# Hybrid attention and state-space trunk: states in the ring of attention outputs, states made one half projection sooner, the last two input tiles by token halves, gate inputs loaded through the ring

## The chip, the core and the metric

The kernel runs on one core of one Trainium2 chip. The core has a matrix engine (TensorE, PE in the profile, with its weight loads as PEld), a vector engine (VectorE, DVE), a scalar engine (ScalarE, ACT), a general engine (GpSimd, POOL) and a queue that here issues every DMA (SyncE, SP). Each engine takes its own instructions in the order in which they stand in its queue; they wait for each other by semaphores. The metric is the device time of one execution in microseconds (us), the median of several runs. One execution is also taken by the hardware profiler; all start times below count from the beginning of its span.

## The reference

Two decoder layers on x of 1024 tokens by 1024 channels in float32, the first with dilated window attention, the second with a state space layer. The change lies in the second:

```python
def s5_mixer(h, w_in, a_re, a_im, log_dt, b_re, b_im, c_re, c_im, d_skip, w_glu, b_glu, w_out):
    proj = h @ w_in
    u, z = proj[..., :SSM_WIDTH], proj[..., SSM_WIDTH:]
    y = s5_scan(u, a_re, a_im, log_dt, b_re, b_im, c_re, c_im, d_skip)
    g = jax.nn.gelu(y)
    y = g * jax.nn.sigmoid(g @ w_glu + b_glu)
    return (y * jax.nn.silu(z)) @ w_out
...
x = x + rms_norm(h, ssm_post_norm[j])
```

`s5_scan` is a linear recurrence over the tokens with 64 complex states for each of 64 groups of 16 channels.

## The kernel before

Matrix products are made in float32 accuracy from two rounded parts of each operand: a helper, `split` (line 80), casts a tile to its high part on ACT (L86) and subtracts that from the tile on another engine, mostly DVE (L87), for the low part. Each product is then three matmuls (`proj_part`, L113): high by high, high by low, low by high.

The second layer has three stages. **Input projection with the state space work** (`layer1`): the projection has 16 column tiles of weights (0 to 7 give `u`, 8 to 15 give `z`), each for two halves of 512 tokens. A half projection is 24 matmuls into one bank of PSUM (`psj`); 32 of them are made in a row by `in_order`. Between them the code interleaves the state space work of 8 groups, each 128 channels wide, by a table: a list `at` gives for each half projection t the stages to be run behind it. The stages of a group e are: its loads (`ssm_loads`: BT, Cg, Sg), the load of its input U from DRAM, where the projection's halves were written (`ssm_input`), of the taps and CA (`ssm_taps`), the states (`ssm_states`) and the outputs (`ssm_outputs`). `ssm_states` makes 8 matmuls `pv` (L1380), then on DVE and POOL a rotation (L1381 to L1384), a scan along the blocks (L1387), and a rotation back (L1389 to L1393) into X. `ssm_outputs` makes 16 matmuls `py` from U with the taps (L1407) and X with CA (L1408), then the gelu on ACT, POOL and DVE (L1409 to L1414, all named Y) and writes Y to DRAM (`y_dr`, L1415). A tile X holds half a group; its pool has two buffers for the tag, so one group's states.

**The gate projection** (`glu`): g is read back from `y_dr`, with tokens and channels in other places, in 16 loads `gy` (8 groups by two token halves, L1476), each split into its high and low part: `g0b` is the first half's pair of tiles, `g1b` the second half's. The loads take their places from a ring of small buffers (`slot`). Then 8 column tiles of `w_glu` by two halves are made. `in_order` begins this stage with a block (start="block"): two weight tiles by two halves in four banks (`psb`), seven of eight groups deep first, the eighth at the end. The weights of a tile are loaded, cast (`whi`) and subtracted (`wlo`) two tiles ahead, since there are two buffers of each.

**The output projection** with the norm and the residual (`out_tiles`).

Large tiles have tags b0 to b5, each a buffer that is used again: `h1` (the normalised input of the layer) is in b4 and b5 for the first token half, in b0 and b2 for the second; the taps are in b1 (groups 0 to 3) and b3 (4 to 7); g is in b1 and b3 for the first half, in b4 and b5 for the second. The ring of attention outputs (pool `outs`, tag O) has four buffers of 128 by 1024 values; in the second layer only the last norm's weights (`post`) use it.

A scheduler sets each engine's order from the order of the code, from priorities (`high_priority`) and from its own clock; `issue_after` holds an instruction behind another one.

Of the kernel before, what the change touches and what calls it, by code (L numbers as in the profile page):

```python
# [15 lines left out]
F32 = mybir.dt.float32  # L16
# [7 lines left out]
P = 128  # L24
S = 1024
D = 1024
KT = 8
H = 512
# [88 lines left out]
def proj_half(c, w, h):  # L117

    pool, tag = ((c.psj, "psj"), (c.pst, "pst"))[c.banks % 2]
    c.banks += c.wide  # L120
    ps = pool.tile([P, H], F32, tag=tag, name="psj")
    proj_part(c, ps, w, h, range(KT))
    return ps
# [643 lines left out]
def in_order(c, srcs, h, use, after=None, start=None, ws=()):  # L767

    t = 0

    def one(e, th, ps):
        nonlocal t
        use(e, th, ps)
        if after:
            after(t)
        t += 1

    ws = list(ws) or [load_w(c, srcs[e]) for e in range(2 if start else 0)]  # L780
    if start == "block":
        jobs = [(e, th) + ((c.psj, "psj"), (c.psl, "psl"))[th] for th in range(2) for e in range(2)]
        pss = [pool.tile([P, H], F32, tag=tag, name="psb") for _, _, pool, tag in jobs]
        for ks in (range(KT - 1), (KT - 1,)):
            for ps, (e, th, _, _) in zip(pss, jobs):
                proj_part(c, ps, ws[e], h[th], ks)
                if ks[0]:
                    one(e, th, ps)
    elif start == "half":
        for e in range(2):  # L790
            one(e, 0, proj_half(c, ws[e], h[0]))
        pss = [c.psj.tile([P, H], F32, tag="psj", name="psj") for _ in range(2)]
        for part in range(2):
            cs = slice(part * 256, part * 256 + 256)
            for e in range(2):
                proj_part(c, pss[e][:, cs], ws[e], [x[:, :, cs] for x in h[1]], range(KT), part == 0)
                if part:
                    one(e, 1, pss[e])
    c.wide = 1 if start == "half" else c.wide
    for e in range(len(ws), len(srcs)):  # L800
        w = load_w(c, srcs[e])
        for th in range(2):
            one(e, th, proj_half(c, w, h[th]))
    c.banks = c.wide = 0

# [562 lines left out]
def ssm_states(self):  # L1368

    c, et, BT, Cg, Sg = self.c, self.et, self.BT, self.Cg, self.Sg  # L1370
    nc = c.nc
    U = self.U
    lo, hi = slice(0, 64), slice(64, 128)
    self.X = []
    for b in range(2):
        gs = slice(b * 4, b * 4 + 4)
        T1, T2, X = (c.ssm.tile([P, 4, P], F32, name=n, tag=n, bufs=2) for n in ("T1", "T2", "X"))
        pv = c.psl.tile([P, 4, P], F32, tag="psl", name="pv")
        for j in range(4):
            nc.tensor.matmul(pv[:, j, :], BT[:, b * 4 + j, :], U[:, b * 4 + j, :], start=True, stop=True)  # L1380
        nc.vector.tensor_tensor(T1, Cg[:, gs], pv, op=ALU.mult)  # L1381
        nc.vector.tensor_tensor(T2[lo], Sg[lo, gs], pv[hi], op=ALU.mult)
        nc.vector.tensor_tensor(T2[hi], Sg[hi, gs], pv[lo], op=ALU.mult)
        nc.gpsimd.tensor_tensor(T1, T1, T2, op=ALU.add)  # L1384
        for j in range(4):
            g = et * 8 + b * 4 + j
            nc.vector.tensor_tensor_scan(T1[:, j], c.rho[:, g:g + 1].to_broadcast([P, P]),  # L1387
                                         T1[:, j], 0.0, op0=ALU.mult, op1=ALU.add)
        nc.gpsimd.tensor_tensor(X[:, :, 1:P], Cg[:, gs, 0:P - 1], T1[:, :, 0:P - 1], op=ALU.mult)  # L1389
        nc.gpsimd.memset(X[:, :, 0:1], 0.0)  # L1390
        nc.vector.tensor_tensor(T2[lo], Sg[lo, gs], T1[hi], op=ALU.mult)
        nc.vector.tensor_tensor(T2[hi], Sg[hi, gs], T1[lo], op=ALU.mult)  # L1392
        nc.vector.tensor_tensor(X[:, :, 1:P], X[:, :, 1:P], T2[:, :, 0:P - 1], op=ALU.subtract)  # L1393
        self.X.append(X)


def ssm_outputs(self):
# [20 lines left out]
def y_view(c, et, th):  # L1418

    return bass.AP(c.y_dr.tensor, c.y_dr.offset + et * P * S + th * 4 * 16384, [[P, P], [16384, 4], [1, P]])  # L1420


def layer1(c, a, h1, ws):

    nc, tc = c.nc, c.tc
    c.ssm = c.es_pa.enter_context(tc.tile_pool(name="ssm", bufs=1, side="left", reuse_waits="tile"))
    def use_u(et, th, ps):
        ut = c.slot("ut")
        with tc.high_priority(AHEAD):
            nc.scalar.copy(ut.rearrange("p (i n) -> p i n", i=4)[:, ::-1, :], ps.rearrange("p (i n) -> p i n", i=4))  # L1430
            dst = bass.AP(c.u_dr.tensor, c.u_dr.offset + et * P * S + (1 - th) * 4 * 16384, [[P, P], [16384, 4], [1, P]])
            nc.sync.dma_start(dst, ut.rearrange("p (i n) -> p i n", i=4))

    def use_z(et, th, ps):
        z = c.slot("z1")
        with tc.high_priority(AHEAD):
            nc.scalar.activation(z, ps, AF.Tanh, scale=0.5)
            nc.vector.scalar_tensor_tensor(z, z, 1.0, ps, op0=ALU.add, op1=ALU.mult)
            nc.sync.dma_start(c.z_dr[et, :, th * H:th * H + H], z)

    groups = [Ssm(c, a, e) for e in range(8)]
    c.taps = []
    at = [[] for _ in range(40)]
    for e in range(8):
        t = (11 * e + 2) // 4
        for stage, d in ((ssm_loads, (-1, 2)[e] if e < 2 else 3), (ssm_input, 5), (ssm_taps, 6), (ssm_states, 7), (ssm_outputs, 10)):
            at[t + d + 1].append((stage, e))

    def run(t):
        for stage, e in at[t + 1]:  # L1450
            if stage is ssm_loads and e == 1:
                with tc.issue_after(groups[0].load_U.ins):
                    stage(groups[e])
            else:
                stage(groups[e])

    def use(e, th, ps):
        (use_u if e < 8 else use_z)(e % 8, th, ps)

    run(-1)  # L1460
    in_order(c, [a["ssm_w_in"][e] for e in range(16)], h1, use, run, start="half", ws=ws)
    for t in range(32, 39):
        run(t)


def glu(c, a):
    nc, tc = c.nc, c.tc
    bh = c.cst.tile([P, KT], F32, name="bh")
    nc.sync.dma_start(bh, a["b_glu"])
    nc.vector.tensor_scalar(bh, bh, 0.5, None, op0=ALU.mult)  # L1470
    g, y2 = [], []
    for th, tags in enumerate((("b1", "b3"), ("b4", "b5"))):
        g.append([c.pb.tile([P, KT, H], F32R, tag=t, name=f"g{th}{t}") for t in tags])
        for et in range(8):
            y = c.slot("gy")
            nc.sync.dma_start(y.rearrange("p (i n) -> p i n", i=4), y_view(c, et, th))  # L1476
            split(c, g[th][0][:, et, :], g[th][1][:, et, :], y)
    y2.append([c.pb.tile([P, KT, H], F32R, tag=t, name=f"y0{t}") for t in ("b0", "b2")])

# [16 lines left out]
def trunk(tc, a):  # L1496
# [6 lines left out]
    with ExitStack() as es:  # L1503
# [51 lines left out]
                          z112.rearrange("p (k x) -> p k x", k=8))  # L1555
        h1, ws = attn_out(c, a, g, raw)
        c.es_pa.close()
        layer1(c, a, h1, ws)
        c.es_pa.close()
        c.pa2 = c.es_pa.enter_context(tc.tile_pool(name="pa2", bufs=1, side="left", reuse_waits="tile"))  # L1560
        y2 = glu(c, a)

        w = [[c.pa2.tile([P, KT, H], F32R, tag=f"w0{x}", name=f"wf0{x}") for x in "hl"],
             [c.pb.tile([P, KT, H], F32R, tag=t, name=f"wf1{t}") for t in ("b1", "b4")]]
# [99 lines left out]
```

## Time and profile before

| what | us |
|---|---|
| median of 3 runs (1678.32 to 1683.48) | 1678.59 |
| the profiled execution's own time | 1679.3 |
| its span | 1677.5 |
| first layer, and the start of the second: 0 to 1250 (PE busy) | 1250 (1239.88) |
| projection before the first states: 1250 to 1298 (PE busy) | 48 (46.83) |
| projection with states and outputs: 1298 to 1480 (PE busy) | 182 (178.51) |
| first block of the gate projection: 1480 to 1512 (PE busy) | 32 (27.87) |
| rest of the gate projection: 1512 to 1581 (PE busy) | 69 (68.67) |
| output projection and the end: 1581 to 1677 (PE busy) | 96 (88.37) |

PE's instructions overlap: a matmul of 512 columns is shown as 0.4 us long, and the next one begins 0.23 us after it, so a hole in PE is read best from starts. A row of the profile such as "PE py L1408 <- DVE X L1393: 2.4, 1, 2.4" says that PE waited before its instructions of line 1408 for X of line 1393 on DVE: us in total, times, longest. Buffer numbers are left out of names, so T1 and T2 are T, Y1 and Y2 are Y, g0b1 and g0b3 are g0b. The granted clock of PE (PEclk) is 1 at full speed.

### The profile page before, as it was taken

Reading aid. Unit: us, or ns where it says so; the run is one execution under the profiler, and the core shown is the slowest. Engines: PE = TensorE matmul, PEld = TensorE weight load, DVE = VectorE, ACT = ScalarE, POOL = GpSimd, SP = SyncE. Lnnn points to the kernel's source line nnn. Section 1 sums busy time; section 2 is a strip of 40 time slices with the busy share of each in tenths; the row PEclk is TensorE's granted clock in tenths of the full one; section 3 lists DMA queues with packets and bytes.
Section 4 is the critical chain, followed back from the end, with each engine's and each line's share of the span. In section 5 each row is a group of like instructions: output and inputs, shape, how many; then the busy total and the mean of one; then the engine's idle time right before and its main releaser. Section 6 shows DMA issues by size and latency. Waiting matters only on the chain.

```text
span 1677.5 us, 26337 instructions
## 1 busy us (share of the span) xinstructions
PE 1650.1 (98%) x9714; PEld 1390.6 (83%) x9714; DVE 1011.9 (60%) x2509; ACT 712.2 (42%) x1730; POOL 460.0 (27%) x303
## 2 busy tenths in 40 slices
PE   8999999999999999999999999999999999999998
PEld 6889999978888888888888888887788887867886
DVE  8698898625554554545455455557562888845533
ACT  5232223236455464645546464654452223343411
POOL 2000000131241514324161441404220344513121
PEclk9999999999999999999999999999999999989999
DMA  6213455531232414233252423318346979365432
GB/s 238 86 49 109 144 181 158 170 109 55 79 99 82 119 54 114 68 90 95 67 139 65 120 79 87 109 34 234 103 162 175 273 222 259 101 207 171 144 120 86
DMA packets 176857, 212.19 MB, mean 126 GB/s; under 512 B 37443, under 2 KB 133462, under 8 KB 176728
## 3 DMA queue, kind: packets, MB, share of 16 engines
q1 hardware_dynamic: 176728, 210.52, 42.3%
q8 instruction: 76, 1.25, 0.3%
q14 instruction: 53, 0.43, 0.1%
HBM read 153.51 MB, written 56.96 MB: 125 GB/s over the span
## 4 chain that ended last, share of the span: by engine, by line
PE 87%; DVE 7%; DMA 3%; issue 1%; POOL 1%; ACT 1%; SPq 0%; DVEq 0%; ACTq 0%; POOLq 0%
PE psj L113 46%; PE psq L376 11%; PE psl L474 5%; PE pso L551 4%; PE pt L502 4%; PE pso L886 3%; PE pso L885 3%; PE pso L884 3%; PE pso L577 1%; PE psb L113 1%; DVE T L1387 1%; PE psv L237 1%; DVE T L1392 1%; PE psv L236 1%; PE psv L235 1%
## 5 line engine op out<-in xcount | busy, mean ns | idle before, releaser
L113 PE MATMUL psj<-hh,wlo 128*128 128x512 f32 x896 | 358.2, 400 | 0.0
L113 PE MATMUL psj<-hh,whi 128*128 128x512 f32 x896 | 358.1, 400 | 0.0
L113 PE MATMUL psj<-hl,whi 128*128 128x512 f32 x896 | 355.2, 396 | 0.0
L87 POOL TENSOR_TENSOR wlo<-wraw,whi 128x1024 fp32r<-128x1024 f32 x48 | 115.2, 2399 | 395.9 <-ACT whi L86 380.8
L113 PEld LDWEIGHTS psj<-hh,whi 128*128 128x128 f32 x896 | 168.8, 188 | 37.0
L113 PEld LDWEIGHTS psj<-hh,wlo 128*128 128x128 f32 x896 | 168.8, 188 | 36.4
L113 PEld LDWEIGHTS psj<-hl,whi 128*128 128x128 f32 x896 | 168.7, 188 | 36.3
L491 ACT ACTIVATE lg<-lg,nm 128x128 f32<-128x128 f32 (+1 forms) x384 | 168.2, 442 | 37.3 <-DVE nm L486 37.3
L480 DVE CUSTOM_DVE_ANT_0 lg<-psl,T 128x128 f32<-128x128 f32 (+1 forms) x384 | 110.5, 347 | 88.7 <-PE psl L474 88.7
L86 ACT CAST whi<-wraw 128x1024 fp32r<-128x1024 f32 x80 | 83.7, 1046 | 163.8 <-PE psj L113 117.5
L376 PE MATMUL psq<-whi,v 128*128 128x256 f32 x640 | 120.3, 284 | 0.0
L87 DVE TENSOR_TENSOR ph<-pt,ph 128x512 fp32r<-128x512 f32 (+2 forms) x160 | 96.7, 622 | 15.3 <-ACT ph L86 13.1
L113 PE MATMUL psj<-h1h,whi 128*128 128x512 f32 (+1 forms) x272 | 105.0, 387 | 0.9 <-ACT h1h L86 0.9
L87 DVE TENSOR_TENSOR kl<-psj,kh 128x512 fp32r<-128x512 f32 x48 | 33.2, 692 | 120.1 <-ACT kh L86 119.5
L113 PE MATMUL psj<-h1l,whi 128*128 128x512 f32 (+1 forms) x272 | 104.1, 383 | 0.2 <-DVE h1l L87 0.2
L113 PE MATMUL psj<-h1h,wlo 128*128 128x512 f32 (+1 forms) x272 | 104.1, 383 | 0.0
L86 ACT CAST ph<-pt 128x512 fp32r<-128x512 f32 (+2 forms) x160 | 81.6, 530 | 46.5 <-PE pt L502 45.5
L376 PEld LDWEIGHTS psq<-whi,v 128*128 128x128 f32 x640 | 100.0, 189 | 1.2 <-issue 1.2
L376 PE MATMUL psq<-wlo,v 128*128 128x256 f32 x320 | 91.2, 286 | 0.7 <-DVE wlo L87 0.7
L551 PE MATMUL pso<-ph,vs 128*128 128x256 f32 (+1 forms) x544 | 86.6, 284 | 0.0
L502 PE MATMUL pt<-identr,lg 128*128 128x128 f32 x560 | 82.2, 276 | 0.0
L1253 POOL TENSOR_TENSOR Ks<-Ks,O 128x16 f32<-128x16 f32 x8 | 3.7, 462 | 284.0 <-ACT Ks L1251 284.0
(284 smaller groups left out, 3688.6 us busy)
## 6 DMA issues: line engine op xcount, KB each, us to landing
wraw<-in_w_in_dram SPq DMA_DIRECT2D x56, 512.0 KB
mw<-wt_dr SPq DMA_DIRECT2D x48, 256.0 KB
v<-in_w_v_dram SPq DMA_DIRECT2D x20, 512.0 KB
vp<-v_dr SPq DMA_DIRECT2D x16, 512.0 KB
wraw<-in_ssm_w_in_dram SPq DMA_DIRECT2D x16, 512.0 KB
v_dr<-v SPq DMA_DIRECT2D x30, 256.0 KB
rot_dr<-rt SPq DMA_DIRECT2D x48, 128.0 KB
ca_dr<-ca SPq DMA_DIRECT2D x32, 144.0 KB
```

What stands on the lines that cost most here:

```text
L86: c.last_hi = nc.scalar.copy(hi, src).ins
L87: return (engine or nc.vector).tensor_tensor(lo, src, f32(hi), op=ALU.subtract)
L113: nc.tensor.matmul(ps, a[:, s], b[:, k, :], start=first and k == 0 and n == 0, stop=k == KT - 1 and n == 2, skip_group_check=True)
L376: nc.tensor.matmul(o, r[x][:, k, ts], w[y][:, k, :], skip_group_check=True, start=i in (0, 4, 5) and t % 2 == k == n == 0, stop=k == 3 and ...
L474: nc.tensor.matmul(psl[:, h, o], x[HEADS[h], qs], y[HEADS[h], ks], start=j == js[0] and n == 0, stop=n == 2, skip_group_check=True)
L480: nc.vector.tensor_tensor_reduce(lg[:, h, j, 0:w], psl[:, h, o], bt[:, h, 256 - w:256], scale=1.0, scalar=-3.0e38, op0=ALU.add, op1=ALU.ma ...
L491: nc.scalar.activation(lg[:, h, j, 0:w], lg[:, h, j, 0:w], AF.Exp, bias=nm[:, h, b:b + 1], accum_out=ms[:, col:col + 1])
L502: c.nc.tensor.transpose(pt[:, n * P:(n + 1) * P], lg[:, h, j, part * P:part * P + P], c.ident)
L551: nc.tensor.matmul(o, l, r, start=n == 0, stop=n == len(jobs) - 1, skip_group_check=True)
L884: nc.tensor.matmul(ps, gh[:, k, ts], wh[:, k, :], start=n == 0, stop=False)
L885: nc.tensor.matmul(ps, gh[:, k, ts], wl[:, k, :], start=False, stop=False)
L886: nc.tensor.matmul(ps, gl[:, k, ts], wh[:, k, :], start=False, stop=n == KT - 1)
```

## The change

Four edits. X of a group becomes one buffer of the ring of attention outputs (both halves of the group in it), so up to four groups' states can stand at once. In the table, the input's load and the states of groups 1 to 7 move one half projection up. `in_order` makes the last two tiles of the input projection by token halves: both tiles' first half, then both tiles' second. And the 16 loads `gy` go through three buffers of the ring of attention outputs, six places, held behind the last group's load of U; g gets other buffers: b1 and b4 for the first half, b5 and b3 for the second.

```diff
@@ in_order
-    c.wide = 1 if start == "half" else c.wide
-    for e in range(len(ws), len(srcs)):
+    c.wide = int(start == "half")
+    pairs = 2 if start == "half" else 0
+    for e in range(len(ws), len(srcs) - pairs):
         w = load_w(c, srcs[e])
         for th in range(2):
+            one(e, th, proj_half(c, w, h[th]))
+
+    ws = [(e, load_w(c, srcs[e])) for e in range(len(srcs) - pairs, len(srcs))]
+    for th in range(2):
+        for e, w in ws:
             one(e, th, proj_half(c, w, h[th]))
@@ ssm_states
-    self.X = []
+
+    X2 = c.outs.tile([P, D], F32, tag="O", name="X", bufs=4).rearrange("p (b g n) -> p b g n", b=2, g=4)
+    self.X = [X2[:, b] for b in range(2)]
     for b in range(2):
         gs = slice(b * 4, b * 4 + 4)
-        T1, T2, X = (c.ssm.tile([P, 4, P], F32, name=n, tag=n, bufs=2) for n in ("T1", "T2", "X"))
+        T1, T2 = (c.ssm.tile([P, 4, P], F32, name=n, tag=n, bufs=2) for n in ("T1", "T2"))
+        X = self.X[b]
...
-        self.X.append(X)
@@ layer1
-        for stage, d in ((ssm_loads, (-1, 2)[e] if e < 2 else 3), (ssm_input, 5), (ssm_taps, 6), (ssm_states, 7), (ssm_outputs, 10)):
+        for stage, d in ((ssm_loads, (-1, 2)[e] if e < 2 else 3), (ssm_input, 4 + (e == 0)), (ssm_taps, 6),
+                         (ssm_states, 6 + (e == 0)), (ssm_outputs, 10)):
...
+    return groups[7].load_U.ins
@@ glu
-    for th, tags in enumerate((("b1", "b3"), ("b4", "b5"))):
+    ring = [x[:, n * H:n * H + H] for x in (c.outs.tile([P, D], F32, tag="O", name="gy", bufs=4) for _ in range(3)) for n in range(2)]
+    for th, tags in enumerate((("b1", "b4"), ("b5", "b3"))):
         g.append([c.pb.tile([P, KT, H], F32R, tag=t, name=f"g{th}{t}") for t in tags])
         for et in range(8):
-            y = c.slot("gy")
-            nc.sync.dma_start(y.rearrange("p (i n) -> p i n", i=4), y_view(c, et, th))
+            y = ring[(8 * th + et) % 6]
+            with tc.issue_after(last_input):
+                nc.sync.dma_start(y.rearrange("p (i n) -> p i n", i=4), y_view(c, et, th))
             split(c, g[th][0][:, et, :], g[th][1][:, et, :], y)
```

What moves, engine by engine. First PE, at the second group's `pv`. Before, it stands behind the last outputs `py` of the first group:

```order
L1408 MATMUL py<-X,CA 128x128
L1407 MATMUL py<-U,taps 128x128
L1408 MATMUL py<-X,CA 128x128
L1380 MATMUL pv<-U,BT 128x128 x8
L113 MATMUL psj<-h1h_12778,whi 128x512
```

and now behind a half projection, the second after the first group's `pv` (h1h_12778 is the second token half's high part, h1h_12324 the first's):

```order
L113 MATMUL psj<-h1h_12778,whi 128x512
L113 MATMUL psj<-h1l_12779,whi 128x512
L113 MATMUL psj<-h1h_12778,wlo 128x512
L1389 MATMUL pv<-U,BT 128x128 x8
L113 MATMUL psj<-h1h_12324,whi 128x512
```

The first group's outputs then come one half projection later, behind the second group's `pv`. For all groups but the first, four half projections now lie between `pv` and `py` (two pairs of them around outputs in the last group).

Second, the SP queue at the end of the input projection. Before (Y_14745 and Y_14763 are group 6's, Y_14845 and Y_14863 group 7's; z_14912 and z_14941 belong to the last two half projections):

```order
L1415 DMA y_dr<-Y_14745 128x512
L1415 DMA y_dr<-Y_14763 128x512
L1439 DMA z_dr<-z_14812 128x512
L98 DMA wraw<-in_w_glu_dram 128x1024
L1439 DMA z_dr<-z_14841 128x512
L1415 DMA y_dr<-Y_14845 128x512
L1415 DMA y_dr<-Y_14863 128x512
L1476 DMA gy<-y_dr 128x4x128 x3
L1439 DMA z_dr<-z_14912 128x512
L1476 DMA gy<-y_dr 128x4x128 x6
```

and now (Y_14737 and Y_14755 are group 6's; z_14704 and z_14733 are tile 13's two halves, z_14810 tile 14's first):

```order
L1488 DMA gy<-y_dr 128x4x128 x4
L1447 DMA z_dr<-z_14704 128x512
L98 DMA wraw<-in_w_glu_dram 128x1024
L1447 DMA z_dr<-z_14733 128x512
L1488 DMA gy<-y_dr 128x4x128 x2
L1423 DMA y_dr<-Y_14737 128x512
L1423 DMA y_dr<-Y_14755 128x512
L1447 DMA z_dr<-z_14810 128x512
L1488 DMA gy<-y_dr 128x4x128 x4
L966 DMA post<-in_ssm_post_norm_dram 128x1024
```

Six of the loads moved ahead of group 6's writes, and seven more stand ahead of group 7's, which follow three rows further on; the first half's load of group 7 follows behind them and behind the next gate tile's weights, and the second half's loads of groups 7 and 5 end the list.

Third, ACT's queue at the same place. Before, the casts of g begin behind everything of the groups (Y_14846 and Y_14864 are group 7's tanh):

```order
L1413 ACTIVATE Y_14846<-Y_14846 128x512
L1413 ACTIVATE Y_14864<-Y_14864 128x512
L1437 ACTIVATE z_14912<-psj 128x512
L86 CAST g0b_14952<-gy 128x512 x3
L86 CAST whi<-wraw 128x1024
L1437 ACTIVATE z_14941<-psj 128x512
L86 CAST g0b_14952<-gy 128x512
L86 CAST g1b_14986<-gy 128x512 x2
```

and now they stand between the pieces of the last two groups (Y_14756 is the tanh of group 6's second half, Y_14843, Y_14844, Y_14861 and Y_14862 are group 7's):

```order
L86 CAST g0b_14947<-gy 128x512
L1421 ACTIVATE Y_14756<-Y_14756 128x512
L86 CAST g0b_14947<-gy 128x512
L1445 ACTIVATE z_14810<-psj 128x512
L1445 ACTIVATE z_14839<-psj 128x512
L1417 ACTIVATE Y_14843<-py 128x512
L1418 ACTIVATE Y_14844<-py 128x512
L86 CAST g0b_14947<-gy 128x512
L1417 ACTIVATE Y_14861<-py 128x512
L1418 ACTIVATE Y_14862<-py 128x512
L86 CAST g1b_14973<-gy 128x512 x2
L1421 ACTIVATE Y_14844<-Y_14844 128x512
```

Behind these follow another cast of g, the second tanh of group 7, one more cast, and then the cast `whi` of the first gate tile. On DVE the low part of tile 15's weights (`wlo`) stands directly behind the last instruction of group 7's states.

More of the change, by code (lines that the diff above doesn't have):

```diff
@@ L1463, in layer1, with glu @@
         run(t)
-def glu(c, a):
+    return groups[7].load_U.ins
+def glu(c, a, last_input):
     nc, tc = c.nc, c.tc
@@ L1557, in trunk @@
         c.es_pa.close()
-        layer1(c, a, h1, ws)
+        last_input = layer1(c, a, h1, ws)
         c.es_pa.close()
         c.pa2 = c.es_pa.enter_context(tc.tile_pool(name="pa2", bufs=1, side="left", reuse_waits="tile"))
-        y2 = glu(c, a)
+        y2 = glu(c, a, last_input)
         w = [[c.pa2.tile([P, KT, H], F32R, tag=f"w0{x}", name=f"wf0{x}") for x in "hl"],
```

## The prediction

> **What bounds the kernel now.** I read the head of the page first, then who the matrix engine waited for, then the stretches of time where it did, then its single instructions there.
>
> ```profile
> PE 1650.1 (98%) x9714; PEld 1390.6 (83%) x9714; DVE 1011.9 (60%) x2509; ACT 712.2 (42%) x1730; POOL 460.0 (27%) x303
> ...
> PE py L1408 <- DVE X L1393: 2.4, 1, 2.4
> ...
> PE psb L113 <- ACT g1b L86: 1.4, 1, 1.4
> PE psb L113 <- ACT whi L86: 1.3, 1, 1.3
> PE psb L113 <- ACT g0b L86: 1.1, 2, 0.6
> PE py L1408 <- POOL Y L1412: 1.1, 1, 1.1
> ```
>
> TensorE (PE) is busy 98% of the span, so nothing is gained by making another engine faster; only PE's own holes count. The change touches the second layer alone (from about 1250 us), and there the list of waits has two kinds of hole: outputs `py` waiting for states `X`, and the first gate block `psb` waiting for its inputs `g0b`, `g1b` and a weight tile `whi`. The first kind, on PE's own rows (start, length, in brackets the idle time before and who ended it):
>
> ```profile
> 1400.77 0.38 PE L1407 MATMUL py<-U,taps 128*128 128x128 f32 x2
> 1403.59 0.49 PE L1408 MATMUL py<-X,CA 128*128 128x128 f32 x2 [2.44 <-DVE X L1393]
> ...
> 1407.04 1.95 PE L1380 MATMUL pv<-U,BT 128*128 128x128 f32 x16
> ...
> 1425.70 0.38 PE L1407 MATMUL py<-U,taps 128*128 128x128 f32 x2
> ...
> 1429.27 1.95 PE L1380 MATMUL pv<-U,BT 128*128 128x128 f32 x16
> ...
> 1464.50 0.38 PE L1407 MATMUL py<-U,taps 128*128 128x128 f32 x2
> 1465.94 0.46 PE L1408 MATMUL py<-X,CA 128*128 128x128 f32 x2 [1.05 <-POOL Y L1412]
> ...
> 1469.28 0.48 PE L113 MATMUL psj<-h1h,whi 128*128 128x512 f32 x1
> ```
>
> An undisturbed group of outputs takes 1429.27 - 1425.70 = 3.57 us. The fourth group took 6.27 and the last 4.78: **2.7 and 1.2 us lost**. The view names POOL for the last one, but the states of that group, on DVE, ended at the same moment (below). The second kind of hole, in the windows (busy time of PE, PEld, DVE, ACT, POOL, granted clock, DMA share, GB/s) and the chain of waits:
>
> ```profile
> 1484.00:1486.00 2.00, 1.88 (x3) 0.79 (x3) 1.94 (x3) 1.14 (x3) 0.00 (x0) 0.53 0.76 216
> ...
> 1492.00:1494.00 2.00, 2.00 (x6) 1.52 (x6) 0.08 (x1) 0.62 (x1) 0.00 (x0) 0.50 1.17 301
> ...
> 1496.00:1498.00 2.00, 2.00 (x10) 1.61 (x9) 0.51 (x1) 0.56 (x1) 0.00 (x0) 1.00 0.13 34
> ...
> 1300.83 16.86 PE psj L113 x72
> ...
> 1475.64 0.70 DVE Y L1414
> ...
> 1477.20 4.43 DMA gy<-y_dr
> 1481.65 0.63 ACT g0b L86
> 1482.30 0.70 DVE g0b L87
> ...
> 1480.37 0.40 PE L113 MATMUL psj<-h1h,wlo 128*128 128x512 f32 x1
> ...
> 1512.68 0.73 PE L113 MATMUL psj<-g0b,whi 128*128 128x512 f32 x2 [0.20 <-ACT whi L86]
> ```
>
> The first gate block is 96 matmuls (four banks of 24). At 16.86/72 = 0.234 us each they need 22.5 us. PE's last projection matmul starts at 1480.37 and ends its slot at 1480.6; the first matmul after the block starts at 1512.68: 32.1 us, so **9.6 us lost**. The chain says why: the last `Y` is written at 1476.4, only then do the 16 loads `gy` stand in SP's queue, each 4.43 us to land, and each followed by a cast and a subtraction. Part of the loss is clock: it falls to 0.53 in 1484 to 1486 and stays at 0.50 to about 1494, when PE issues 6 matmuls in 2 us instead of 10.
>
> **The states, one half projection sooner.** No work is added. X moves from two small buffers of the layer's pool, which allow one group at a time, to the ring of attention outputs, so a group's states need not wait for the outputs before it. In the new order between a group's `pv` and its `py` there lie four half projections with a `py` and mostly a `pv`, or about 4 x 5.62 + 3.57 + 1.9 = 28 us (5.62 is a third of 16.86; 1.9 a `pv`, by the row at 1407.04), where mostly three halves lay, about 17. What is needed: DVE's rows for the last group, then some windows and one load's issue.
>
> ```profile
> 1448.18 0.68 DVE L1381 TENSOR_TENSOR T<-Cg,pv 128x512 f32<-128x512 f32 x1
> ...
> 1458.86 1.19 DVE L87 TENSOR_TENSOR wlo<-wraw,whi 128x1024 fp32r<-128x1024 f32 x1
> ...
> 1464.09 2.35 DVE L1393 TENSOR_TENSOR X<-X,T 128x508 f32<-128x508 f32 x2
> ...
> 1300.00:1320.00 20.00, 20.00 (x103) 16.70 (x102) 16.15 (x22) 3.58 (x6) 6.22 (x6) 1.00 1.07 268
> ...
> 1400.00:1420.00 20.00, 17.56 (x100) 15.03 (x100) 17.92 (x27) 5.58 (x9) 9.76 (x10) 1.00 0.97 265
> ...
> 1460.00:1480.00 20.00, 18.95 (x98) 15.81 (x98) 11.88 (x14) 7.00 (x12) 9.41 (x9) 1.00 0.53 165
> ...
> 1295.65 0.43 SPq L1365 DMA_DIRECT2D U<-u_dr  x1
> ```
>
> From 1448.18 to 1466.4 is 18.3 us for a group, a weight tile and one `z` included. 28 covers 18.3 with 9 to spare, more than the two waits together: I take the whole **2.7 + 1.2 = 3.9 us**. Ends of the range: 0 (they stay) and 3.9 (PE cannot win more there).
>
> **Tiles 14 and 15 by token halves, and the loads through the ring.** The matmuls are the same 96; their order is 14 first half, 15 first half, outputs of group 7, 14 second half, 15 second half. So the first token half of `h1` is free 11.2 us (two halves) before the block, and the tiles in its place can be filled: `g0b`'s low part and `g1b`'s high part. Seven of the eight loads of the first half no longer stand behind the last `Y`. The same 16 casts (0.63 ACT) and 16 subtractions (0.70 DVE) are issued, about 10 and 11 us; some move ahead of the block, beside projections: in 1460 to 1480 DVE is busy 11.88 and ACT 7.00 of 20 us, which leaves room for them.
>
> Does it come in time? Call the new start of the block T0: 1480.6 - 3.9 = 1476.7. I follow the queues by hand with durations quoted above and those of this chain:
>
> ```profile
> 1467.07 2.06 DMA y_dr<-Y
> ...
> 1469.23 0.60 ACT Y L1409
> 1469.83 0.50 ACT Y L1410
> ...
> 1473.18 1.77 POOL Y L1412
> ...
> 1474.97 0.64 ACT Y L1413
> ...
> 1511.58 1.06 ACT whi L86
> ```
>
> (a) Group 7's `pv` starts at T0 - 6 x 5.62 - 2 x 3.57 - 1.9 = 1433.9. DVE first finishes group 5's `Y`: its outputs end one half earlier, at 1428.3, and by the rows above `Y` follows the end of the outputs by 7.1 (1469.2 to 1476.3): 1435.4. Then 18.3 plus another `z` of 0.6 for the states: 1454.3; then the low part of tile 15's weights, 1.2: 1455.5. PE asks for it at T0 - 3 x 5.62 - 3.57 + 0.5 = 1456.8 (the tile's third matmul). **1.3 us to spare.** (b) SP's next load, a gate tile's weights, waits for that low part, and the fifth `gy` stands behind it: issued 1456.3, landed 1460.7, cast 1461.4. The last tanh of group 6 stands behind that cast on ACT: 1462.0, `Y` on DVE 1462.7, written 1465.1 with its issue, seventh `gy` landed 1469.8, cast 1470.5. Group 7's second `Y` stands behind it: two ACT (1.1), POOL (0.6 + 1.77), tanh 0.64: 1474.6; one more cast, and the first gate tile's `whi` at 1475.2 + 1.06 = 1476.3. **0.4 us to spare** before T0. (c) The last but one load, group 5 of the second half, takes over the place of group 7's first half, which is issued behind another weight load: landed about 1482.3, cast and subtracted 1483.6; then 4.43 and 0.63: 1488.9. PE's order asks for it after some 55 matmuls: 1476.7 + 12.9 = 1489.6. **0.7 us to spare.**
>
> By hand then nothing is late, but with under 1.5 us in three places, each estimate good to perhaps 2 us. The block's loss has 0 and 9.2 us as its ends (of the 9.6, 0.4 is the wait for the third weight tile at the block's end, whose cause, PE itself, stays). I take 1.0, near the low end, because every row says just in time. Where the cover goes, each us is PE's.
>
> Edits at nothing: the last norm's weights are loaded near the end of this layer and not before it; they are used after the gate projection, whose 14 halves behind the block (14 x 5.62 = 79 us) hide the load.
>
> **Sum.** Own time of the profiled execution 1679.3 (span 1677.5, 1.8 around it): 1679.3 - 3.9 - 9.2 + 1.0 = 1667.2. The median of the runs, 1678.6, lies 0.7 below it: **1666.5**. Less than 0.3% (5 us) is about what a measurement cannot tell from no change.
>
> **Rivals.** *A, a rest of the stall, with its clock.* (b) slips by 3 us: PE stops 2 to 3 us at the block's start in pieces. Row for: the clock fell in 1484 to 1486 after pieces of idle time of 1.3 us and less. Ten us at 0.50 cost up to 5 us. About 2.5 + 4 = 6.5 in place of 1.0: 1672. Against: at T0 the first pieces lie ready, which they did not at 1480.6. Chance 0.16.
> The Trainium skill ("TensorE: Matmul & The Clock Gate", Part 1) says that the clock is halved after a whole idle window of about 3.4 us. The 2.44 us wait at 1403.59 in a window of clock 1.00 agrees; the fall at 1484 does not, since no idle piece before it comes near 3.4. By the page A would cost its 2.5 alone, 1668.
> *B, the states' waits were DVE's load, not buffers.* The wait then moves with them: 3.9 back, 1670.4. For: DVE busy 17.92 of 20 in the stretch of the long wait. Against: 9 us of room. Chance 0.07.
> *C, the change does not do what it says for the block:* loads issued sooner stand behind SP's waits for weights and `Y`, and the block loses its 9.2 again: 1674.7. For: SP takes its queue in order. Against: the first four loads stand ahead of the last two groups' `Y` in the new queue. Chance 0.09.
> *D, slower: the transfers of the states.* Inputs asked for one half (5.62 us) sooner meet a DMA share of 1.07 in 1300 to 1320. If it can deliver nothing sooner, each of the first groups' `pv` waits up to 5.62 us: three of them 16.9, 1666.5 + 16.9 = 1683.4. It decides once `pv` waits total 12 us. Against: the second `U` is issued at 1295.65, 16 us ahead of the new second `pv` (1300.83 + 2 x 5.62 = 1312.1). Chance 0.06.
>
> **Numbers.** Forecast (1664 to 1669) 0.62, A 0.16, B 0.07, C 0.09, D 0.06. The range goes from 1664 (no rest at all, 1665.5, and the 0.4 and a run's spread) to 1675 (A, B and C), leaving D and a little more out. Faster by over 0.3% (below 1673.6): forecast, B and most of A, 0.82; within: C and the rest of A, 0.12; slower: D, 0.06.
>
> **What would show it.** States: no `py` row waits for `X`, every group of outputs 3.57 us. Block: `psb` from start to the next `psj` about 23 us, clock 1.00 throughout. (a) wrong: a `psj` of tile 15 waiting for `wlo`; (b): `psb` waiting for `whi` or `g0b`; (c): `psb` waiting for `g1b` half-way. D: DVE `T` or PE `pv` waiting for DMA near 1310 to 1350. The prediction is wrong if new holes on PE in the second layer sum to over 7 us.

## The result and the profile after

The changed kernel takes 1671.8 us (median of five; 1671.36 to 1674.69) where the kernel before takes 1678.59 (1677.96 to 1683.48) on the same chip: by these medians 6.8 us less, where 12.1 were forecast. The ratio on record is 0.9945, 95% interval 0.9932 to 0.9958; it is not the quotient of the two medians (0.9960), and by itself it would be 7 to 11 us less. So the kernel is faster, since the interval leaves 1 out, but whole times give the size of the gain to within some 2 us only. The profiled execution has a span of 1672.9 us, after 1677.5.

The head of the page, and the rows of PE's waits in the second layer, of the changed kernel:

```profile
PE 1646.8 (98%) x9714; PEld 1389.2 (83%) x9714; DVE 1024.4 (61%) x2509; ACT 709.7 (42%) x1730; POOL 471.4 (28%) x303
...
PE psb L113 <- ACT whi L86: 2.6, 1, 2.6
PE psj L113 <- DVE wlo L87: 1.9, 1, 1.9
```

The waits of `py` for X are gone, and so are those of the gate block `psb` for `g0b` and `g1b`. Two others stand in their place: one before the block for its first weight tile `whi`, one in the input projection for the low part `wlo` of a weight tile. PE's single rows give the places, with the first `pv` and the first `psj` behind the block as marks:

```profile
1300.90 1.95 PE L1389 MATMUL pv<-U,BT 128*128 128x128 f32 x16
...
1460.64 0.50 PE L113 MATMUL psj<-h1h,wlo 128*128 128x512 f32 x1 [1.87 <-DVE wlo L87]
...
1480.47 0.40 PE L113 MATMUL psj<-h1h,wlo 128*128 128x512 f32 x1
1483.52 0.73 PE L113 MATMUL psb<-g0b,whi 128*128 128x512 f32 x2 [2.65 <-ACT whi L86]
...
1508.17 0.73 PE L113 MATMUL psj<-g0b,whi 128*128 128x512 f32 x2 [0.31 <-ACT whi L86]
```

The same first mark in the kernel before (its second, at 1512.68, stands with the prediction):

```profile
1298.88 1.95 PE L1380 MATMUL pv<-U,BT 128*128 128x128 f32 x16
```

**The stretch between the two marks is the measure of everything below.** It holds the same 1056 matmuls in each kernel here and all that the change touches. Before it is 1512.68 - 1298.88 = 213.80 us, now 1508.17 - 1300.90 = 207.27: 6.5 us less. The start of the first mark differs by 2.0 us between these two executions, by what lies ahead of the stretch; it differs by 1.2 between two executions of the changed kernel itself (below), and among all profiled executions here it lies between 1298.5 and 1302.9, and from the second mark to the start of PE's last matmul it is 156.2 to 156.3 us in every one. Without any hole the stretch would be 213.8 - 2.7 - 1.2 - 9.6 = 200.3. Of the 7.0 us that are left, 2.0 are at tile 15's `wlo` and 5.0 in the block: 2.8 for `whi`, about 1.6 of half clock behind it, 0.5 for the third weight tile.

Why tile 15's `wlo` came late stands in the rows of POOL, ACT and DVE (the Y at 1438.72 are group 5's, X and T before them group 6's states; T and X from 1441.25 on are group 7's):

```profile
1429.56 1.73 POOL L1398 TENSOR_TENSOR X<-Cg,T 128x508 f32<-128x508 f32 x1 [1.05 <-DVE T L1396]
...
1433.99 1.58 POOL L1398 TENSOR_TENSOR X<-Cg,T 128x508 f32<-128x508 f32 x1 [1.66 <-DVE T L1396]
1435.52 1.72 POOL L1420 TENSOR_TENSOR Y<-Y,Y 128x512 f32<-128x512 f32 x1
1437.32 0.94 POOL L1419 TENSOR_SCALAR Y<-Y 128x512 f32<-128x512 f32 x1
1438.35 1.60 POOL L1420 TENSOR_TENSOR Y<-Y,Y 128x512 f32<-128x512 f32 x1
...
1437.27 0.63 ACT L1421 ACTIVATE Y<-Y 128x512 f32<-128x512 f32 x1 [5.67 <-POOL Y L1420]
...
1429.46 0.69 DVE L1400 TENSOR_TENSOR T<-Sg,T 64x512 f32<-64x512 f32 x1
...
1434.45 1.66 DVE L1400 TENSOR_TENSOR T<-Sg,T 64x512 f32<-64x512 f32 x1
...
1437.89 0.91 DVE L1402 TENSOR_TENSOR X<-X,T 128x508 f32<-128x508 f32 x1
1438.72 2.61 DVE L1422 SCALAR_TENSOR_TENSOR Y<-Y,Y 128x512 f32<-128x512 f32 x2
1441.25 0.68 DVE L1390 TENSOR_TENSOR T<-Cg,pv 128x512 f32<-128x512 f32 x1
...
1457.44 1.59 DVE L1402 TENSOR_TENSOR X<-X,T 128x508 f32<-128x508 f32 x1
1458.96 1.62 DVE L87 TENSOR_TENSOR wlo<-wraw,whi 128x1024 fp32r<-128x1024 f32 x1
```

The states of group 6, now made sooner, hold POOL until 1435.5, and most of the gelu of group 5 follows behind them there. On DVE they stand ahead of group 5's Y too: the tanh was done at 1437.9, but Y begins only behind group 6's last X, at 1438.7, and its two pieces are finished at 1441.3. From 1429.5 on to `wlo` DVE has no idle piece over 0.2 us. Its own instructions stretch where POOL works beside them: L1400 takes 0.69 us at 1429.46, just before POOL begins an X, and 1.66 at 1434.45, begun while POOL makes the other one. Why `whi` came late stands in the rows of SP and ACT:

```profile
1474.21 0.44 SPq L966 DMA_DIRECT2D post<-in_ssm_post_norm_dram  x1
1474.75 0.38 SPq L1488 DMA_DIRECT2D gy<-y_dr  x1
...
1481.90 0.62 ACT L86 CAST g1b<-gy 128x512 fp32r<-128x512 f32 x1 [3.57 <-DMA gy<-y_dr]
1482.42 1.04 ACT L86 CAST whi<-wraw 128x1024 fp32r<-128x1024 f32 x1
```

and in the chain of waits, which has that load from its issue to its landing:

```profile
1474.75 7.13 DMA gy<-y_dr
```

The cast `whi` stands behind the cast of the eleventh load, and that load needs 7.13 us, behind the 512 KB of the last norm's weights. These weights are first used at 1600, in the output projection.

### The profile page after: what moved, and what is told of

The parts are those of the page before. It is cut to its first block, busy times and chain, and to the rows that moved or that the text cites. A ratio compares the mean times of both kernels' runs of the same rounds, so it can differ in the third digit from the quotient of the medians.

```text
span 1672.9 us, 26320 instructions
## 1 busy us (share of the span) xinstructions
PE 1646.8 (98%) x9714; PEld 1389.2 (83%) x9714; DVE 1024.4 (61%) x2509; ACT 709.7 (42%) x1730; POOL 471.4 (28%) x303
## 4 chain that ended last, share of the span: by engine, by line
PE 84%; DVE 9%; DMA 3%; POOL 2%; issue 1%; ACT 1%; SPq 0%; DVEq 0%; ACTq 0%; POOLq 0%
PE psj L113 45%; PE psq L376 10%; PE psl L474 5%; PE pso L551 4%; PE pt L502 4%; PE pso L892 3%; PE pso L891 3%; PE pso L890 3%; DVE T L1396 2%; PE psb L113 1%; PE pso L577 1%; DVE T L1401 1%; DMA gy<-y_dr 1%; DVE wlo L87 1%; PE psv L237 1%
```

## The experiments

Each kernel was compared with the kernel before on one chip; the ratio is the one on record, not the quotient of the medians. The edit of e1 is shown against the kernel before, all others against the changed kernel. Marks, waits and the block are read from its profile: the idle time of PE before `py` for X and before `psj` for tile 15's `wlo` from the view of waits; the loss of the block from the start of the last `psj` ahead of it, plus 0.23 and the 22.5 us of its 96 matmuls, to the second mark.

| kernel | median us (before) | ratio, 95% interval | stretch | py for X | wlo of tile 15 | block |
|---|---|---|---|---|---|---|
| before | | 1 | 213.80 | 3.5 | none | 9.6 |
| the change | 1671.8 (1678.6) | 0.9945, 0.9932 to 0.9958 | 207.27 | none | 1.9 | 5.0 |
| e1 states only | 1675.6 (1682.4) | 0.9966, 0.9955 to 0.9977 | 208.81 | none | none | 8.7 |
| e2 loads only | 1678.8 (1682.4) | 0.9982, 0.9971 to 0.9993 | 211.19 | 2.4 | 3.3 | 1.3 |
| e3 tanh first | 1672.9 (1682.4) | 0.9951, 0.9935 to 0.9967 | 206.79 | none | 1.9 | 4.4 |
| e4 wlo on POOL | 1675.1 (1682.4) | 0.9962, 0.9950 to 0.9973 | 207.13 | none | none | 6.8 |
| e5 whi first | 1674.7 (1682.4) | 0.9951, 0.9934 to 0.9969 | 209.09 | none | 2.3 | 6.4 |
| e6 whi first, wlo on POOL | 1676.2 (1682.4) | 0.9969, 0.9956 to 0.9982 | 208.85 | none | none | 8.6 |
| e7 the change again | 1673.4 (1682.4) | 0.9948, 0.9934 to 0.9963 | 207.25 | none | 1.9 | 4.9 |
| e8 post late | 1673.5, one time (1682.4) | | 206.29 | none | 1.9 | 2.4 |
| e9 eight places, whi first | 1671.8 (1682.1) | 0.9938, 0.9923 to 0.9953 | 203.63 | none | 1.9 | 1.3 |
| e10 as e9, wlo on POOL | 1671.4 (1682.1) | 0.9937, 0.9920 to 0.9954 | 204.01 | none | none | 3.7 |
| e11 old place of states | 1679.4, one time (1682.1) | | 210.35 | 1.3 | 2.0 | 6.2 |
| e12 tiles in order | 1670.8 (1681.4) | 0.9941, 0.9923 to 0.9960 | 202.52 | none | none | 2.4 |

The repeat e7 puts the stretch at 207.25 after 207.27, where the intervals of whole times are 2 to 3 us wide on either side. But there is one trace of each kernel, and in these two the half clock behind the block's wait also fell on the same place, 183.3 us behind the first mark. Whether a wait draws such a stretch depends on its place (last section), so 1.6 us more or less in the stretch may be chance. PE's idle time in the stretch, added up from the gaps between its starts, is free of that: 10.2 us before, 5.6 in the change and 5.5 in e7, 6.2 in e5, 4.5 in e8, 3.4 in e9, 3.7 in e10, 2.4 in e12.

### The two halves of the change, each alone

e1 is the kernel before with X in the ring and the states one half projection sooner; tiles and loads as before.

```diff
+    X2 = c.outs.tile([P, D], F32, tag="O", name="X", bufs=4).rearrange("p (b g n) -> p b g n", b=2, g=4)
...
+(ssm_input, 4 + (e == 0)), (ssm_taps, 6), (ssm_states, 6 + (e == 0)), (ssm_outputs, 10)
```

> Only the states' part of the change: X in the ring of attention outputs, input's load and states one half projection sooner; tiles 14 and 15 in the old order, gate inputs loaded as before. Measure: the stretch from the first pv to the first psj behind the gate block, 213.8 us before, 207.3 with the whole change. My forecast's term (the py waits are one of buffers, 3.9 us): stretch 209.9, no py wait, gate block 9.6 us lost as before, about 1674.7 us in all. Rival (DVE is full there, the wait only moves, as the 1.9 us wait of tile 15's matmuls for wlo in the changed kernel suggests): stretch 211.5 to 213.8, a new psj wait for wlo of about 2 us or the py waits back.

No `py` waits, and no wait for `wlo` came in their place: up to the last `psj` the stretch is 177.43 us after 181.49, 4.06 us less. The forecast's term holds. The block then still loses 8.7.

e2 is the other half: the order of tiles 14 and 15 and the ring of loads, the states as before.

```diff
-    X2 = c.outs.tile(...)
+        T1, T2, X = (c.ssm.tile([P, 4, P], F32, name=n, tag=n, bufs=2) for n in ("T1", "T2", "X"))
...
+(ssm_input, 5), (ssm_taps, 6), (ssm_states, 7), (ssm_outputs, 10)
```

> Only the gate's part: tiles 14 and 15 by token halves and the loads through the ring; the states as before, in their own pool and at their old place. If the rest of the stall in the changed kernel (about 5 us with its clock) comes from the loads' own chain, it is here too: stretch 213.8 - 9.2 + 4.6 = 209.2, about 1674. If it comes from the states made sooner (they push group 5's outputs and then tile 15's wlo back on DVE), the gate block loses about 1 us: stretch 205.6, about 1670, and this part alone beats the whole change.

Both theories were wrong about the sum, and the second right about the block: it loses only 1.3 us. But PE waits before it. The waits of PE in this kernel:

```profile
PE psj L113 <- DVE wlo L87: 3.3, 1, 3.3
PE py L1415 <- DVE X L1400: 2.4, 1, 2.4
```

With the half clock behind these two (3.41 us at 0.50 after each) the gain of 8.2 in the block shrinks to 2.6 in the stretch. The wait for tile 15's `wlo` belongs to the new order of the tiles: it asks for these weights one half projection sooner. The two halves then do not add up: 5.0 alone and 2.6 alone, 6.5 together.

### Which queue makes the block late

e3 moves one cast on ACT: the fifth load's behind the second tanh of group 6.

```diff
-            with tc.issue_after(last_input):
+            with tc.issue_after(last_input), tc.issue_after(c.tanh[6 if 8 * th + et > 3 else 0]):
                 nc.sync.dma_start(y.rearrange("p (i n) -> p i n", i=4), y_view(c, et, th))
-            split(c, g[th][0][:, et, :], g[th][1][:, et, :], y)
+                split(c, g[th][0][:, et, :], g[th][1][:, et, :], y)
```

> The changed kernel, with the fifth load's cast of g behind the second tanh of group 6 on ACT (in the changed kernel it stands ahead, waits for its load until 1466.3, and that tanh, ready at 1461.7, waits with it). Theory: this inversion holds Y of group 6, its write, the seventh load and, through the subtractions queued on DVE behind that Y, the ring's places. Undone, the block's wait for whi (2.65 us) and the half clock (about 1.7 us) go: stretch 203 to 204, about 1667.5; the 1.9 us wait for tile 15's wlo stays. Rival (the late load, 7.1 us to land behind the norm's 512 KB and four others, is the DMA's): the block's start waits 2 us or more as before, stretch 206 to 207.5.

The stretch is only 0.5 us shorter, as the rival had it: the theory fell. The second write of group 6's Y was issued 4.5 us sooner, counted from the first mark, but on SP the write of a `z` stands ahead of the seventh load, and that `z` stood on ACT behind the same two casts.

e4 makes the low part of tile 15's weights on POOL.

```diff
-    ws = [(e, load_w(c, srcs[e])) for e in range(len(srcs) - pairs, len(srcs))]
+    ws = [(e, load_w(c, srcs[e], e == 15 and c.nc.gpsimd)) for e in range(len(srcs) - pairs, len(srcs))]
```

> The changed kernel, with the low part of tile 15's weights made on POOL in place of DVE; it stands behind the two multiplications of group 7's states there and ahead of group 6's gelu, which moves 2.4 us back. Theory (tile 15's wait is DVE's queue): the 1.9 us wait for wlo goes; the gate tile's weights and the fifth load are issued about 1.6 us sooner, so the block starts sooner too, but still waits for whi, 2 to 3 us: stretch 205.0, about 1669.5. Rival (the root of the block's stall too): both go, stretch 202 to 203. If POOL cannot take it, psj waits for wlo as before or py for X.

The wait for `wlo` is gone, so it was DVE's queue; but the stretch is 207.13, where 205.0 was expected. The block now waits 4.5 us for `whi` where it waited 2.6: its inputs come when they come, and PE only waits elsewhere.

e5 puts `whi` of the first gate tile ahead of the third and fourth casts of the second half.

```diff
+            ws, hi = ([load_w(c, a["w_glu"][0])], c.last_hi) if (th, et) == (1, 2) else (ws, hi) if th else (None, None)
...
+            with tc.issue_after(hi or last_input):
+                split(c, g[th][0][:, et, :], g[th][1][:, et, :], y)
...
-    in_order(c, [a["w_glu"][e] for e in range(8)], g, use, start="block")
+    in_order(c, [a["w_glu"][e] for e in range(8)], g, use, start="block", ws=ws + [load_w(c, a["w_glu"][1])])
```

> The changed kernel, with the cast whi of the first gate tile ahead of the casts of the second half's third and fourth loads on ACT. Undoing the tanh's place gave only 0.5 us, because the write of z behind the same casts still held the seventh load; so what starts the block late is read anew: whi stands behind a cast whose load lands 6.7 to 7.1 us after its issue, though its own weights lie ready. Theory (only the place of whi on ACT): the block starts with no wait and full clock, 2.8 + 1.6 us less, stretch 202.9, about 1667.5 on the first chip's scale. Rival (the loads themselves are late, PE then waits for g1b or g0b a few matmuls later): stretch 205 to 207, psb waiting for g1b.

> Both edits that each take one wait away: whi of the first gate tile ahead of those casts, and the low part of tile 15's weights on POOL. Alone the second moved its 2 us into the block (the wait for whi grew from 2.8 to 4.7). Theory (the two losses share the chain: the block's start is bound by the loads, so the first needs the second and the reverse): stretch 202.9 - 2.0 = 200.9, only some 0.5 us of PE's idle time left in it. Rival: the block's inputs come at a time of their own, stretch as in the run with whi first alone.

e6 is e5 with the edit of e4. Both are longer than the change by the stretch; by whole times neither is told from it. In e5 the rival was right in kind: PE waits for `g1b`. Its 209.09 lies 2 us above the rival's range, since two stretches of half clock follow, where the change has one; by PE's idle time alone e5 is 0.6 us worse than the change. In e6 the rival was right too (208.85, as e5). In e5 the block starts at once and then stops after 13 us; in e6 it waits 0.7 us for `whi`, and then 3.2 for `g1b`. PE's wait in e5, from the view of waits:

```profile
PE psb L113 <- ACT g1b L86: 2.6, 1, 2.6
```

and what the chain of waits has ahead of it, the load and its cast:

```profile
1487.72 6.80 DMA gy<-y_dr
1494.52 0.02 issue
1494.55 0.63 ACT g1b L86
```

This is the last load of all, the second half's of group 5. It takes the place in the ring that the first half's load of group 7 held, which waits for the last Y. In the change no wait for this load shows, since the block starts late.

> The changed kernel again, on the chip of these runs, as their yardstick: stretch 207.3 as before, with 2.0 us for tile 15's wlo, 2.8 for whi and one window of half clock.

It came out so: 207.25, with waits of 1.9 us for `wlo` and 2.6 for `whi` by the view, and one stretch of half clock.

e8 puts the load of the norm's weights behind the eleventh load.

```diff
-    c.nc.sync.dma_start(t, bass.AP(src.tensor, src.offset, [[0, P], [1, D]]))
+    with c.tc.issue_after(c.last_gy or c.last_hi): c.nc.sync.dma_start(t, bass.AP(src.tensor, src.offset, [[0, P], [1, D]]))
...
+                load = nc.sync.dma_start(y.rearrange("p (i n) -> p i n", i=4), y_view(c, et, th)); c.last_gy = load.ins if 8 * th + et < 12 else c.last_gy
```

> The changed kernel, with the load of the last norm's weights (512 KB) behind the eleventh load of g, not just ahead of it. If that transfer is why the eleventh load lands 7.1 us after its issue, it lands 1.5 to 2 us sooner and whi with it: stretch about 204.5 to 205.5 (less clock lost too). If the load waits for the four before it in the DMA queues, stretch 207 as before.

SP and ACT in e8:

```profile
1474.15 0.36 SPq L1488 DMA_DIRECT2D gy<-y_dr  x1
1474.60 0.46 SPq L966 DMA_DIRECT2D post<-in_ssm_post_norm_dram  x1
...
1478.16 0.62 ACT L86 CAST g1b<-gy 128x512 fp32r<-128x512 f32 x1 [0.18 <-DMA gy<-y_dr]
1478.68 0.63 ACT L1421 ACTIVATE Y<-Y 128x512 f32<-128x512 f32 x1
1479.22 1.04 ACT L86 CAST whi<-wraw 128x1024 fp32r<-128x1024 f32 x1
```

The eleventh load lands 4.0 us after its issue (1478.14 - 1474.15) in place of 7.1, `whi` is ready 3.0 us sooner, counted from the first mark, before PE asks, and the block starts with no wait. So the transfer ahead of the eleventh load is what made the start late; the edit changed nothing else by intent, but this is one trace, and the order on ACT moved with it (the eleventh cast ahead of the last tanh), which is not told apart. The stretch, 206.29 where 204.5 to 205.5 was expected, is only 1 us shorter, since PE then waits 1.2 us for the last load, and since the wait for `wlo`, no longer than before, drew about 1.6 us of half clock this time.

### Taking the waits out together

e9 gives the ring a fourth buffer, so that each second half's load follows the first half's of its own group, with `whi` first as in e5. e10 adds the edit of e4.

```diff
-bufs=4) for _ in range(3)) for n in range(2)]
+bufs=4) for _ in range(4)) for n in range(2)]
...
-            y = ring[(8 * th + et) % 6]
+            y = ring[et]
```

> As the run with whi first, and the ring with four buffers, eight places, so that a place passes from the first half's load of a group to the second half's of the same group. With six places the second half's load of group 5 takes the place of the first half's of group 7, which cannot be issued before the last Y; with whi first PE waited 2.8 us for that load's cast, and ran 6.8 us at half clock. Theory (that place is the bound of the block): no psb wait, clock 1.00 in the block, only tile 15's wlo wait of 2.0 to 2.4 left: stretch 202.7 to 203.1. Rival (the loads at the end are held by the DMA queues or SP, not by the place): psb waits for g1b again, stretch 206 to 209.

> As the run before with tile 15's low part on POOL too. Theory: all three waits go, stretch 200.9, or 201.8 with the 0.9 us for whi that this place of wlo left in the earlier run; about 6 us less than the changed kernel. Rival: with the block another 2 us earlier its inputs are late again, stretch 203 or more with psb waits for g0b or g1b.

e9 does nearly what its theory asks: no wait in the block but 0.2 us, full clock, stretch 203.63, 3.6 less than the change. So the ring's place was the second limit: the last load is now group 7's, which PE needs last. The load of the norm's weights also moved here, behind the seven loads at 1471.9; but e8, where it moved with six places, still waited for the last load. e10 wins nothing more: PE comes 2 us sooner and waits 2.7 us for `whi`; the stretch is its rival's, but not the tile that is waited for.

e11 leaves the change as it is but puts the states back to their old place in the table.

```diff
-(ssm_input, 4 + (e == 0)), (ssm_taps, 6), (ssm_states, 6 + (e == 0)), (ssm_outputs, 10)
+(ssm_input, 5), (ssm_taps, 6), (ssm_states, 7), (ssm_outputs, 10)
```

> The changed kernel with the inputs' load and the states at their old place in the table; X stays in the ring of attention outputs. It tells the two halves of the states' edit apart. Before, POOL waited 30.6 us for py at the filling of X's first columns, with the gelu and the rotation behind it. If the ring alone took the py waits away: no py wait, stretch 209 or less, tile 15's wlo wait 3 to 3.5 us as in the loads' part alone. If the earlier place is what counts: py waits for X of 2 us or more, stretch 210 to 211.

It came between the two. POOL's waits in the kernel before, from 1298 to 1480, had this row:

```profile
POOL X L1390 <- PE py L1408: 30.6, 5, 7.5
```

In e11, as in the change, POOL no longer waits for `py`, so the ring takes that away alone. But `py` still waits 1.3 us for X, where it waited 2.4 in e2, with the same order of tiles and X in its old pool: of the long wait the ring takes 1.1 and the earlier place 1.3. The last group's wait, 1.1 us before, can't be divided so, since in both kernels the wait for `wlo` just ahead covers it.

e12 leaves the change as it is but makes tiles 14 and 15 one after the other, as before the change.

```diff
-    pairs = 2 if start == "half" else 0
+    pairs = 0
```

> The changed kernel with tiles 14 and 15 each made for both token halves in turn, as before the change; states and the ring of loads as changed. Theory (the new order costs the wait for tile 15's wlo, one half projection sooner, but without it g's tiles in the place of h1's first half come free only 5.6 us ahead of the block): no wlo wait, block start earlier, more stalls for g1b in it and half clock of 7 us or more, stretch 207.5 to 210. Rival (the order of the tiles only costs): stretch 205 or less, block stalled under 2 us.

The rival was right, and the stretch is the shortest of all, 202.52. In the old order tile 14's weights are done with sooner, which lets `whi` of the first gate tile into their buffer long before the block, and tile 15's `wlo` is asked for later. ACT's cast, and PE's waits around the block, in e12:

```profile
1466.93 1.04 ACT L86 CAST whi<-wraw 128x1024 fp32r<-128x1024 f32 x1
...
PE psb L113 <- ACT g1b L86: 1.1, 1, 1.1
PE psj L113 <- ACT whi L86: 0.3, 1, 0.3
PE psb L113 <- ACT whi L86: 0.2, 1, 0.2
```

Ten loads of g now stand behind the last Y on SP, and the block still loses only 2.4 us. ACT's and SP's orders moved with the tiles (`whi` ahead of the seventh cast, the norm's weights ahead of the last Y), so how much of the 4.7 us each of these makes isn't told apart. By whole times e9, e10 and e12 (0.9938, 0.9937, 0.9941) are not told from the change (0.9945 and 0.9948); by the stretch and by PE's idle time they are.

## Why the prediction was right, and where it was not

**What bounds the kernel.** Right: only PE's own holes counted. In each of these executions the stretch is 200.1 to 200.3 us plus its holes and half clock, and what follows it stays as it was.

**The states, 3.9 us.** Right in size: 4.06 in e1. The cause was half right. The buffers were one part; 1.3 us of the long wait stay with the ring alone and go with the earlier place (e11, one trace). That fits rival B's mechanism, DVE's load, with POOL's and ACT's order beside it; no run separates these.

**The block, 9.2 saved and 1.0 left.** This term was mis-sized, and with it the forecast's own range of 1664 to 1669, held at 0.62, did not come; 1671.8 lies in the range given only because that was drawn out to 1675 for A, B and C. Left are 4.5 in the block (beside the 0.4 to 0.5 for the third tile) and 2.0 ahead of it, 6.5 where 1.0 was said. On the scale of one execution: 1667.2 forecast, 2.0 for the later first mark, 5.5 for this term give 1674.7, which is the profiled execution's own time (the median lies 2.9 below it). Point by point, with 2.0 added to the forecast's times for that mark:

- (a) said that DVE first finishes group 5's Y, at 1437.4. It did at 1441.3. The 7.1 us from the outputs to Y were taken from the last group, where no other group's states stand between; here they were 11. The step overlooked that the edit which makes the states sooner puts group 6's states ahead of group 5's gelu, on POOL and on DVE. Group 7's states then took 17.7 us where 18.9 were said, and `wlo` was ready at 1460.6, 3.1 late, of which 1.3 were cover. The step also took the new order of the tiles as given: in e1 and e12 `wlo` is ready at the same time, 159.7 us behind the first mark, and nobody waits for it. Nor is the place of the states the whole of it: with the old place, in e11, the wait is 2.0.
- (b) said "one more cast", and then `whi`, 0.4 us to spare. `whi` was ready at 1483.5, 2.8 after PE asked for it and 5.2 after the time said (1478.3 on this scale). **The step that failed is the pricing of the load of the norm's weights at nothing.** I asked when these weights are used, and 79 us of cover is right for that. I did not ask what stands behind the transfer: the eleventh load, with the cast of its piece and `whi` behind it. e8 shows the price: 3.0 of the 5.2. The other 2.2 lie earlier in the chain, where (a)'s lateness is, and no run divides them.
- (c) said 0.7 us to spare for the second half's load of group 5. In e5, whose first mark is that of before, it was 2.8 too late for PE. It was issued at 1487.72, some 4 us later than said, and took 6.8 us to land where the 4.43 of the chain of before was used. In the change no wait for it shows, since the block starts later.
- The tiles by token halves were counted as what lets the loads in. e12 shows that they weren't needed for it and that, by the stretch, they cost more than they brought.

**The rivals.** A put the time at 1672 and is what came: `whi` late by about 3 us, with half clock behind. Its parts were not: the clock cost 1.6, where 4 was said, and 2.0 came from (a), so that its sum fits is luck. B's mechanism may hold for half of the long wait (1.3 of 2.4), but the wait didn't move on with the states, as B had it. C: the first four loads, and two more, did come sooner. D: no `pv` waited for its inputs, so the DMA could deliver them.

The clock behind the block's wait, in stretches of 3.41 us (columns as in the prediction's windows), in the change:

```profile
1480.79:1484.20 3.41, 0.76 (x4) 0.59 (x4) 1.39 (x2) 2.30 (x4) 0.00 (x0) 1.00 1.00 339
1484.20:1487.61 3.41, 3.41 (x10) 2.36 (x9) 3.41 (x6) 2.23 (x4) 0.00 (x0) 0.50 0.63 197
1487.61:1491.02 3.41, 3.41 (x16) 2.78 (x15) 0.65 (x2) 0.00 (x0) 0.00 (x0) 1.00 1.02 313
```

PE was busy 0.76 of 3.41 us, then ran one such stretch at 0.50.
The Trainium skill ("TensorE: Matmul & The Clock Gate", Part 1) has the clock halved after an idle window of about 3.4 us, of a counter that runs freely; the length agrees with these rows, where the half clock lasted 3.41 us, but PE's wait was 2.65 us, not the whole of one. By that rule alone no half clock would have followed.

## What to carry to other kernels

Ask of a transfer that is moved not only who waits for it but what is issued behind it: 512 KB that nobody needed for over 100 us cost the block its start. An edit that brings one stage forward brings it ahead of another stage on every in-order queue that both use; follow DVE, POOL and ACT as closely as the engine whose wait is removed. Where several inputs come just in time, taking one wait away shows the next (e4, e5, e10), so measure a stretch between two marks that holds them all, and undo each edit of a bundle alone: here, by the stretch, one of four (the tiles by token halves) was better left out.

## What the runs showed of the chip that was not expected

In these traces the half clock comes on a fixed grid. In each trace with two or more such stretches their starts lie a whole number of 3.413 us apart: in the change 1484.20 and 1668.52, 54.0 times 3.413. Whether a wait costs the clock depends on how it falls into this grid. Two waits for the same `wlo`, 1.9 us each: in the change PE kept 1.88 us of work in the window, and the clock stayed; in e8 it kept 1.51 and lost it. The windows of the change, of e8, and of e10, whose wait of 2.7 us was split by the grid:

```profile
1456.89:1460.31 3.42, 1.88 (x9) 1.17 (x7) 3.32 (x3) 0.63 (x1) 3.25 (x3) 1.00 0.00 0
1460.31:1463.72 3.41, 3.08 (x13) 2.52 (x14) 1.97 (x3) 0.00 (x0) 1.42 (x1) 1.00 0.50 132
```

```profile
1458.04:1461.46 3.42, 1.51 (x7) 0.92 (x6) 3.42 (x4) 0.63 (x1) 3.25 (x3) 1.00 0.03 6
1461.46:1464.87 3.41, 3.41 (x9) 2.67 (x8) 0.61 (x1) 0.00 (x0) 0.07 (x1) 0.50 0.94 279
```

```profile
1477.54:1480.95 3.41, 1.62 (x7) 0.96 (x6) 0.75 (x3) 1.26 (x3) 1.29 (x1) 1.00 0.83 284
1480.95:1484.37 3.42, 2.48 (x10) 1.74 (x11) 3.25 (x6) 3.39 (x6) 0.00 (x0) 1.00 0.81 282
```

Between the two marks of all these traces the clock fell after windows in which PE was busy 0.25 to 1.51 of 3.41 us, and stayed after those with 1.62 and more, but for one (1.84, in e1, the second such window in a row). To come back it asked for more: after a window at 0.50 in which PE was busy 1.57 to 3.02 us another one followed (before, e1, e5, e6, e11), and full clock came only after one with 3.33 and more. A window more at 0.50 costs about 1.6 us, nearly as much as a wait of this length; so a stage that is just in time pays for a small slip once or nearly twice, by its place on the grid.
